# A hybrid HGRN2 / attention / MoE layer: late modulations, the shared expert, the first unit and the order of units

## The chip, the cores and the metric

The kernel runs on one core of one Trainium2 chip. The metric is the device time of one execution in microseconds. Shorter is better.

## The reference

One layer over 256 latent tokens and 256 context tokens of width 1024, all in float32. Only the parts that the change touches matter here:

```python
cond, cond_ctx = silu(c), silu(c_ctx)
mod = cond @ w_ada + b_ada                    # w_ada: 1024 x 6144
sh1, sc1, g1, sh2, sc2, g2 = split(mod, 6)    # 1024 each
h  = modulate(x, sh1, sc1)                    # (LN(x)) * (1 + sc1) + sh1
y  = token_mixer(h, hc, ...)                  # HGRN2 heads, attention heads, merged
x  = layer_norm(alpha * x + g1 * y)
h2 = modulate(x, sh2, sc2)
# 64 experts of width 256, the best 8 per token
routed = sum over experts e: gates[:, e] * (silu(h2 @ Wg[e]) * (h2 @ Wu[e])) @ Wd[e]
shared = (silu(h2 @ w_sh_gate) * (h2 @ w_sh_up)) @ w_sh_down
x  = layer_norm(alpha * x + g2 * (routed + shared))
```

Each expert's weights are 3 MB: gate and up 1 MB each, down 1 MB. The parts of `w_ada` for `g1`, `sh2`, `sc2` and `g2` (4096 columns, 16 MB) are needed late: `g1` after the token mixer, the others from the routing on. They are called the late modulations below.

## The kernel before

**The order on the engines.** TensorE's instructions stand in the order in which the code is written (`manual_schedule`), from the start to the end of the token mixer, and again in the unit loop of the MoE. In the routing between the two, a planner sets TensorE's order, as it does for the other engines everywhere. Weights are loaded by SyncE's queue, in the order of the code; a load waits until its buffer is free.

**The HGRN2 stage** (`Pair`, about 57 to 332 us) works on four pairs of heads. While the scan of one pair runs in small steps (`decays`, `keys`, `states`, `carried`, `squares`, `readout`), the projections of the next pair are fed in between on TensorE (`Feed.pull`). Each projection takes a block of `w_in` of 1024 x 256, which is split into a high part (ScalarE, L335) and a low part (VectorE, L336). Blocks of `w_in` and of the late columns of `w_ada` alternate in the list `todo` and share five buffers of 512 KB (tag `wraw`); a block takes two.

**The late modulations** (`late_sums`, L595) come in 16 chunks of 256 columns, one after each block of a projection. For a chunk ScalarE scales eight pieces of 128 x 256 by `cond` (L601), and GpSimd adds the eight up in three steps (L607 to L609) into `acc`, a tile of 128 x 1024. The sum over the 128 partitions is left to `late_spread` (L611): every four chunks, TensorE multiplies `acc` by ones. For `g1` that is a broadcast to all rows (L617); for the other three it is eight matmuls with one column each (L623), whose stationary operand is a block of `acc` read with a step of eight elements.

In the opening, the early modulations go another way (`ada_parts`, L456): eight narrow matmuls per chunk. Their stationary operand is `cond` of one k, 32 columns wide, and four of them write the four groups of 32 rows of one PSUM bank `pa`, 128 x 256. The sum of the four rows 0, 32, 64 and 96 is the result. The constant `sel2` has a 1 in these rows.

**The routing** (L1141 to L1269) normalizes, transposes and modulates two blocks `t` of 128 tokens, multiplies by the router's weights (L1204), chooses experts on VectorE (`choose`, L1159), ranks the experts by the number of their tokens, and gives each expert a column of its rank. The list `idx` of experts by rank goes to SyncE, which loads weights by it. Four experts (`NSTAT`) stand first whatever their number, so their weights are loaded ahead; they are called static here, the other 60 dynamic.

**The shared expert's gate and up products** (`shared_gu`, L1469) are 16 matmuls for each `t`, two for each of eight k. They are written behind the routing, and the planner may place those of `t` = 0 within it.

**Units.** A unit is up to 128 rows (four tiles of 32) of one or more experts; `_ORDER` (L34) lists the experts of the 29 units. `_program` (L53) writes the steps: `g` gate and up (L1398), `P` places, `t` activation, `G` gather of two units (L1373), `d` down (L1406), `s` and `S` scatter (L1430). The first gather, for unit 0 alone, stands ahead of the shared expert's second half, and unit 0's `g` behind all of the shared expert.

**Slots for weights.** Gate and up weights have six slots in all (`free["g"]`): two for the static ones ahead, two more when the mixer's memory is free, one more when the routing's is, and the shared expert's after its use. An expert holds its slot from its load to the end of the last unit that uses it. `fetch_ahead` (L294) starts the next load in the order of use whenever a slot is given back (`done`, L306).

## Time and profile before

| | |
|---|---|
| Runs of the kernel before | 1134.71, 1138.26, 1138.22 us; median 1138.22 |
| The profiled execution | 1142.01 us, span 1140.1 us |
| Mean granted clock of TensorE | 0.972 |
| Busy share of the span: TensorE, VectorE, ScalarE, GpSimd | 93%, 59%, 40%, 20% |
| HBM read | 293.05 MB, 258 GB/s over the span |

The profiled execution is 3.8 us above the median of the runs, and 1.9 us of its time lie around the span. Busy shares are means over stages with different limits, so they say little by themselves. PE is TensorE, DVE VectorE, ACT ScalarE, POOL GpSimd. A line of the trace gives the kernel's line (L388), the tile written and the tiles read. The text in brackets at the end of a line is the time for which the engine had stood idle before it, and what ended that.

### The profile page before, as it was taken

What the parts mean: (1) busy time and instruction counts of PE and PEld (TensorE: products, weight loads), DVE (VectorE), ACT (ScalarE), POOL (GpSimd) and SP (SyncE); (2) the same over time, 40 slices, a digit from 0 to 9 for tenths busy, and PEclk for the clock granted to TensorE, in tenths of its full rate; (3) what the DMA queues carried; (4) which work ended last, traced back from release to release, by engine and by line L of the source; (5) the groups of instructions that cost most, each with busy time, mean ns of one, the idle gap of its engine ahead of it and who ended that gap; (6) DMA issues with size and microseconds to landing.
All of it is one profiled execution on the core that took longest, in us unless ns stands there. A gap on an engine that the chain in (4) does not pass through costs nothing.

```text
span 1140.1 us, 18936 instructions
## 1 busy us (share of the span) xinstructions
PE 1054.8 (93%) x7232; PEld 735.9 (65%) x7232; DVE 678.0 (59%) x1323; ACT 453.5 (40%) x874; POOL 226.7 (20%) x215
## 2 busy tenths in 40 slices
PE   5998979999899899899998999999998999999994
PEld 3796958879799788788997644444434444454441
DVE  5587695967954786787687333444434344444355
ACT  4584846658543564565533112221112122111120
POOL 1116143342454374460001000000000000000021
PEclk9999989999889999999998899999999899999998
DMA  9944444453576443333695579999999999979991
GB/s 321 295 149 154 143 132 151 126 165 112 183 172 150 114 90 80 89 73 118 232 374 226 222 286 412 399 423 421 425 423 425 422 426 425 423 314 384 426 414 47
DMA packets 115101, 295.36 MB, mean 259 GB/s; under 512 B 7080, under 2 KB 86896, under 8 KB 90432
## 3 DMA queue, kind: packets, MB, share of 16 engines
q1 hardware_dynamic: 113088, 290.46, 67.1%
q0 software_dynamic: 1776, 3.47, 3.3%
q8 instruction: 58, 0.95, 0.3%
q14 instruction: 35, 0.29, 0.1%
q10 hardware_dynamic: 144, 0.20, 0.0%
HBM read 293.05 MB, written 1.05 MB: 258 GB/s over the span
## 4 chain that ended last, share of the span: by engine, by line
PE 48%; DVE 15%; DMA 14%; issue 8%; ACT 6%; POOL 5%; SPq 2%; DVEq 0%; ACTq 0%; POOLq 0%
PE pgu L1398 14%; PE proj L388 10%; PE pdn L1406 6%; DMA gu<-in_w_e_up_dram 5%; PE pxg L1373 4%; DMA gu<-in_w_e_gate_dram 3%; DVE wlo L336 3%; DMA wada<-in_w_ada_dram 3%; DMA G<-in_na_rpb_dram 2%; PE proj L394 2%; PE py L1430 2%; DVE s L728 2%; POOL kl L957 2%; PE pgu L1473 1%; SPq L319 1%
## 5 line engine op out<-in xcount | busy, mean ns | idle before, releaser
L1398 PE MATMUL pgu<-gu,xg 128*32 128x512 f32 (+1 forms) x1456 | 211.7, 601 | 8.8 <-DMA gu<-in_w_e_up_dram 7.3
L336 DVE TENSOR_TENSOR wlo<-wraw,whi 128x1024 fp32r<-128x1024 f32 x102 | 141.8, 1392 | 47.0 <-ACT whi L335 44.9
L1398 PEld LDWEIGHTS pgu<-gu,xg 128*32 128x32 f32 (+1 forms) x1456 | 66.1, 118 | 150.1 <-issue 143.0
L335 ACT CAST whi<-wraw 128x1024 fp32r<-128x1024 f32 x102 | 105.6, 1045 | 47.2 <-PE proj L388 34.5
L1294 DVE SCALAR_TENSOR_TENSOR ac<-ac,gcol,pgu 128x256 f32<-128x256 f32 (+1 forms) x29 | 13.9, 480 | 181.1 <-ACT ac L154 181.1
L1406 PE MATMUL pdn<-dn,at 128*32 128x512 f32 (+3 forms) x740 | 106.0, 589 | 0.0
L388 PE MATMUL proj<-hl,whi 128*128 128x256 f32 (+1 forms) x480 | 103.3, 330 | 0.0
L388 PE MATMUL proj<-hh,whi 128*128 128x256 f32 (+1 forms) x480 | 101.8, 330 | 0.0
L388 PE MATMUL proj<-hh,wlo 128*128 128x256 f32 (+1 forms) x480 | 99.5, 327 | 0.0
L1511 POOL TENSOR_TENSOR end<-cf,mod 128x1024 f32<-128x1024 f32 x1 | 1.9, 1897 | 467.0 <-PE pgu L1398 467.0
L154 ACT ACTIVATE ac<-pgu 128x256 f32<-128x256 f32 (+1 forms) x31 | 11.9, 384 | 203.1 <-PE pgu L1398 203.1
L388 PEld LDWEIGHTS proj<-hh,wlo 128*128 128x128 f32 x480 | 75.8, 193 | 8.8 <-issue 1.4
L388 PEld LDWEIGHTS proj<-hl,whi 128*128 128x128 f32 x480 | 74.3, 193 | 6.6 <-issue 0.7
L388 PEld LDWEIGHTS proj<-hh,whi 128*128 128x128 f32 x480 | 74.1, 191 | 6.9 <-issue 0.5
L1420 ACT CAST rh<-pdn 128x512 fp32r<-128x512 f32 x56 | 32.8, 585 | 101.8 <-PE pdn L1406 94.2
L1421 DVE TENSOR_TENSOR rl<-pdn,rh 128x512 fp32r<-128x512 f32 x56 | 38.6, 691 | 57.6 <-ACT rh L1420 57.5
L1431 DVE TENSOR_TENSOR x<-x,py 128x512 f32<-128x512 f32 x108 | 69.0, 680 | 0.0
L601 ACT ACTIVATE wada<-wada,cond 128x256 f32<-128x256 f32 x128 | 58.5, 500 | 25.1 <-DMA wada<-in_w_ada_dram 25.1
L1406 PEld LDWEIGHTS pdn<-dn,at 128*32 128x32 f32 (+2 forms) x740 | 29.6, 116 | 57.9 <-issue 55.3
L1373 PE MATMUL pxg<-oh,x2h 128*128 128x256 f32 (+1 forms) x240 | 64.1, 302 | 1.4 <-DVE x L1431 1.4
L607 POOL TENSOR_TENSOR wada<-wada 128x1024 f32<-128x1024 f32 x16 | 44.3, 2769 | 97.4 <-ACT wada L601 83.4
L1373 PE MATMUL pxg<-oh,x2l 128*128 128x256 f32 (+1 forms) x240 | 61.3, 289 | 0.0
(389 smaller groups left out, 2030.0 us busy)
## 6 DMA issues: line engine op xcount, KB each, us to landing
gu<-in_w_e_gate_dram SPq DMA_DIRECT2D x64, 1024.0 KB, 15.3
gu<-in_w_e_up_dram SPq DMA_DIRECT2D x64, 1024.0 KB, 17.5
dn<-in_w_e_down_dram SPq DMA_DIRECT2D x61, 1024.0 KB, 17.3
wraw<-in_w_in_dram SPq DMA_DIRECT2D x80, 512.0 KB, 4.6
wada<-in_w_ada_dram SPq DMA_DIRECT2D x48, 512.0 KB, 4.7
wraw<-in_w_branch_a_dram SPq DMA_DIRECT2D x8, 512.0 KB, 3.5
wraw<-in_w_branch_b_dram SPq DMA_DIRECT2D x8, 512.0 KB, 3.8
wraw<-in_w_out_dram SPq DMA_DIRECT2D x8, 512.0 KB, 7.9
```

The costliest lines, as they stand in the source:

```text
L335: nc.scalar.copy(hi, raw)
L336: nc.vector.tensor_sub(lo, raw, hi.bitcast(F32))
L388: nc.tensor.matmul(o, a[:, m * P:(m + 1) * P], b[:, :n], start=first, stop=last)
L394: nc.tensor.matmul(o, b[:, t * P:(t + 1) * P], a, start=first, stop=last)
L601: nc.scalar.activation(w, w, AF.Identity, scale=cond[:, k, 0:1])
L607: nc.gpsimd.tensor_tensor(w0, w0, w1, op=OP.add)
L1373: r = nc.tensor.matmul(pg_, part[:, t, k, :], oh[:, t, :w_], start=(t == 0 and part is x2h), stop=(t == 1 and part is x2l))
L1398: nc.tensor.matmul(o[s:s + w_], xg[:, k, i * P + s:i * P + s + w_], W["g"][j][:, :, k, :], start=(k == 0), stop=(k == KD - 1))
L1406: nc.tensor.matmul(pd[s:s + w_, :ns.stop - ns.start], at[:, jj, s:s + w_], W["d"][j][:, jj, ns], start=(jj == 0), stop=(jj == 1))
L1420: nc.scalar.copy(rh[:used], z)
L1421: last_rl[0] = nc.vector.tensor_sub(rl[:used], z, rh[:used].bitcast(F32)).ins
L1431: nc.vector.tensor_add(to[:, t, ns], to[:, t, ns], py)
```

## The change

The sums of the late modulations go the way of the early ones: eight narrow matmuls into `pa` and one copy by ScalarE per chunk. The three GpSimd additions and the eight ScalarE scalings go. `acc` now has four partial rows instead of 128 partial ones, so the spread uses `quarter`, which is 1 in the rows 0, 32, 64 and 96 and 0 elsewhere, or a column of `sel2`. For the three modulations with one-column matmuls, the copy into `acc` already puts the elements in the order of use, so that the stationary block is contiguous.

```diff
-        w0, w1 = take(None, c)
-        for k in range(KD):
-            w = (w0, w1)[k // 4][:, k % 4, :]
-            nc.scalar.activation(w, w, AF.Identity, scale=cond[:, k, 0:1])
+        pa = ada_parts(take(None, c))
         if c % 4 == 0:
             if c > 8:
                 late_spread()
             sums[1] = pg.tile([P, D], F32, tag="acc", name="acc", bufs=1)
         sums[0] = c
-        nc.gpsimd.tensor_tensor(w0, w0, w1, op=OP.add)
-        nc.gpsimd.tensor_tensor(w0[:, 0:2], w0[:, 0:2], w0[:, 2:4], op=OP.add)
-        nc.gpsimd.tensor_tensor(sums[1][:, c % 4 * 256:(c % 4 + 1) * 256], w0[:, 0], w0[:, 1], op=OP.add)
+        m = c % 4 * 32
+        if c < 12:
+            nc.scalar.copy(sums[1][:, 8 * m:8 * m + 256], pa[:, :256])
+        else:
+            nc.scalar.copy(sums[1].rearrange("p (k m) -> p k m", k=KD)[:, :, m:m + 32],
+                           pa[:, :256].rearrange("p (m k) -> p k m", k=KD))
...
-                nc.tensor.matmul(pr1, ones, acc[:, n * 512:(n + 1) * 512], start=True, stop=True)
+                nc.tensor.matmul(pr1, quarter, acc[:, n * 512:(n + 1) * 512], start=True, stop=True)
...
-                nc.tensor.matmul(pr1[:, k:k + 1], acc.rearrange("p (m k) -> p k m", k=KD)[:, k, :], ones[:, 0:1],
-                                 start=True, stop=True)
+                nc.tensor.matmul(pr1[:, k:k + 1], acc[:, k * P:(k + 1) * P], C("sel2")[:, 0:1], start=True, stop=True)
```

TensorE's written order now runs through the routing too (`order.close()` at its start and the entering behind it are gone). The shared expert's products are written between the routing's own instructions: for `t` = 0 k 0 and 1 behind the first choice, 2 and 3 behind the second block's transposes, 4 to 7 behind the second choice; for `t` = 1 k 0 to 3 in the ranking, and k 4 to 7 behind unit 0's gate and up, which now follows the first gather.

```diff
-    order.close()
     mix.close()
...
+        if t:
+            shared_gu(0, range(2, 4))
         for k in range(KD):
-            on_pe[t] = nc.tensor.matmul(pl[:, t * NE:(t + 1) * NE], h2[k][:, ts], wr[:, k, :], start=(k == 0),
-                                        stop=(k == KD - 1))
+            nc.tensor.matmul(pl[:, t * NE:(t + 1) * NE], h2[k][:, ts], wr[:, k, :], start=(k == 0),
+                             stop=(k == KD - 1))
         choose(t)
+        shared_gu(0, range(4, KD) if t else range(2))
...
+    shared_gu(1, range(1))
     pcn = ps_y()
...
+    shared_gu(1, range(1, 2))
     pix = ps_y()
...
+        if i:
+            shared_gu(1, range(3, 4))
         pj = ps_y() if i else ps_dn()
...
     by_column(0, place, pos)
+    shared_gu(1, range(2, 3))
     by_column(1, gate, gj)
...
-    shared_gu(0, range(3), turned[0].ins)
-    shared_gu(0, range(3, 8), turned[1].ins)
     ohs_ = prepare(0)
-    shared_gu(1, range(8), gather(ohs_))
+    ohg_ = gated(ohs_, 0)
+    gather(ohs_)
+    places(ohg_)
+    outs_ = {0: gate_up(0, ps_dn())}
+    done("g", 0)
+    shared_gu(1, range(4, KD))
     free["g"].append(shs[0])
     fetch_ahead()
-    order.enter_context(tc.manual_schedule(engines={nc.tensor.engine}))
     ats = [act_t(pgs[t], None) for t in range(2)]
-    places(gated(ohs_, 0))
```

The order of the units is new. The static experts 0 to 3 are used in the units 8, 0, 1 and 15 before, and in 10, 3, 0 and 1 after. Expert 4, which has five tiles, is used in the units 21 and 22 before, and in 13 and 20 after. The last unit is the same.

```diff
-_ORDER = [[1, 35], [2, 36], [13, 14], [6, 37], [15, 38, 39], [16, 17], [18, 19], [7, 40], [0, 41], [20, 42, 43], [8, 44], [21, 45, 46], [22, 23], [24, 25], [26, 47, 48], [3, 49], [27, 28], [29, 30], [9, 50], [10, 51], [31, 32], [4], [4, 11], [52, 53, 54, 55], [12, 56], [57, 58, 59, 60], [5], [33, 34], [61, 62, 63]]
+_ORDER = [[2, 35], [3, 36], [13, 37, 38], [1, 39], [6, 40], [14, 15], [16, 41, 42], [17, 18], [19, 43, 44], [20, 21], [0, 45], [22, 46, 47], [23, 24], [4], [25, 26], [7, 48], [27, 28], [29, 30], [31, 32], [33, 34], [4, 8], [9, 49], [10, 50], [51, 52, 53, 54], [11, 55], [56, 57, 58, 59], [5], [12, 60], [61, 62, 63]]
```

## Rows read from the trace of the kernel before

**Rows 1.** Busy time of the engines in the HGRN2 stage and in the units: from:to, length, then the busy us (and instructions) of PE, PEld (weight loads), DVE, ACT and POOL, then the granted clock, the DMA engines' busy share and GB/s.

```profile
56.60:332.00 275.40, 256.45 (x1837) 228.55 (x1836) 215.47 (x341) 183.99 (x389) 105.03 (x76) 0.96 0.47 147
...
656.30:1127.00 470.70, 453.63 (x2997) 204.41 (x2998) 200.61 (x437) 88.22 (x172) 9.10 (x5) 0.99 0.94 391
```

**Rows 2.** Groups of instructions by line, from 56.6 to 332 us: line, engine, operation, tiles, count, then busy us and mean ns of one, then the engine's idle time before them and what ended it.

```profile
L336 DVE TENSOR_TENSOR wlo<-wraw,whi 128x1024 fp32r<-128x1024 f32 x45 | 64.7, 1439 | 16.1 <-ACT whi L335 14.2 <-PE proj L388 1.9
...
L601 ACT ACTIVATE wada<-wada,cond 128x256 f32<-128x256 f32 x128 | 58.5, 500 | 25.1 <-DMA wada<-in_w_ada_dram 25.1
...
L623 PE MATMUL pr<-ones,acc 128*128 128x1 f32 x48 | 11.6, 371 | 0.0
```

**Rows 3.** Waits of TensorE's matmuls from 56 to 332 us: who waited for whom, total us, times, the longest.

```profile
PE psc L749 <- ACT ex L154: 6.6, 3, 4.7
PE pu L775 <- DVE kt L759: 4.6, 3, 2.2
PE pk L745 <- DVE v L691: 3.0, 1, 3.0
```

**Rows 4.** Timeline (start us, length us, what): the split L336 on VectorE once with GpSimd idle, and once beside GpSimd's L607.

```profile
57.69 1.22 DVE L336 TENSOR_TENSOR wlo<-wraw,whi 128x1024 fp32r<-128x1024 f32 x1 [0.17 <-ACT whi L335]
...
109.73 2.38 POOL L607 TENSOR_TENSOR wada<-wada 128x1024 f32<-128x1024 f32 x1 [5.90 <-ACT wada L601]
...
110.62 2.57 DVE L336 TENSOR_TENSOR wlo<-wraw,whi 128x1024 fp32r<-128x1024 f32 x1 [0.62 <-ACT whi L335]
```

**Rows 5.** Busy time of the engines in the four stretches of the HGRN2 stage's time and just behind it in which the granted clock is 0.50 (columns as in rows 1).

```profile
155.47:162.30 6.83, 6.19 (x21) 4.87 (x22) 6.32 (x12) 3.39 (x7) 0.00 (x0) 0.50 1.03 340
216.91:220.32 3.41, 3.41 (x10) 2.62 (x9) 3.41 (x3) 1.03 (x3) 3.16 (x2) 0.50 0.36 119
292.00:298.83 6.83, 4.09 (x24) 4.00 (x25) 6.65 (x14) 4.58 (x9) 0.82 (x2) 0.50 0.56 167
329.55:336.38 6.83, 6.83 (x33) 6.83 (x33) 2.11 (x4) 1.04 (x1) 0.79 (x1) 0.50 0.90 145
```

**Rows 6.** Timeline of TensorE in the opening: two chunks of narrow matmuls (32 instructions) between matmuls of the full width.

```profile
41.97 0.39 PE L539 MATMUL po<-hl,whi 128*128 128x512 f32 x1
42.20 0.40 PE L539 MATMUL po<-hh,wlo 128*128 128x512 f32 x1
42.53 1.93 PE L461 MATMUL pa<-wada,cond 128*32 128x256 f32 x32
44.39 0.51 PE L539 MATMUL proj<-hh,whi 128*128 128x512 f32 x1
```

**Rows 7.** Timeline of TensorE: the spread of one modulation (the stationary blocks have a step), and two matmuls of the MoE with contiguous blocks and what follows them.

```profile
212.75 3.85 PE L623 MATMUL pr<-ones,acc 128*128 128x1 f32 x16
...
777.23 0.38 PE L1357 MATMUL poh<-cf,ohg 128*128 128x128 f32 x2
777.44 0.38 PE L1297 MATMUL pat<-cf,ac 128*128 128x128 f32 x2
```

**Rows 8.** Timeline of TensorE in the routing and up to unit 0: the second block's transposes, the count of tokens per expert (L1222), the first gather, the shared expert's second half, its activation's transposes, unit 0's gate and up.

```profile
617.36 1.04 PE L1194 MATMUL py<-cf,x 128*128 128x128 f32 x8
...
626.08 0.28 PE L1222 MATMUL py<-ones,mask 128*64 128x1 f32 x2 [0.56 <-DVE mask L1180]
...
630.36 0.47 PE L1373 MATMUL pxg<-oh,x2h 128*128 128x128 f32 x1
...
637.25 8.56 PE L1473 MATMUL pgu<-gu,h 128*128 128x256 f32 x32
...
647.29 0.44 PE L1297 MATMUL pat<-cf,ac 128*128 128x128 f32 x2 [1.26 <-DVE ac L1292]
...
656.34 7.18 PE L1398 MATMUL pgu<-gu,xg 128*32 128x512 f32 x64 [1.41 <-issue]
```

**Rows 9.** Timeline of VectorE and ScalarE in the routing: the second block's normalization, its router scores' sigmoid, and the list of experts.

```profile
614.16 1.23 DVE L1188 TENSOR_SCALAR x<-x,mv,rs 128x1024 f32<-128x1024 f32 x1 [0.66 <-POOL rs L189]
...
622.75 0.22 ACT L154 ACTIVATE sco<-pdn 128x64 f32<-128x64 f32 x1 [2.14 <-PE pdn L1204]
...
628.22 0.21 DVE L1244 CAST idx<-py 1x64 int32<-1x64 f32 x1
```

**Rows 10.** The issue of the first dynamic expert's up weights in the timeline of SyncE's queue; then DMA issues (what, queue, count, KB each, median us from issue to landing): that one's (629 to 632.9 us), and those of the late columns of `w_ada` (79 to 130 us).

```profile
630.32 0.34 SPq L241 DMA_DIRECT2D gu<-in_w_e_up_dram  x1
...
gu<-in_w_e_up_dram SPq DMA_DIRECT2D x1, 1024.0 KB, 7.9
...
wada<-in_w_ada_dram SPq DMA_DIRECT2D x7, 512.0 KB, 3.7
```

**Rows 11.** Timeline of TensorE: gate and up of unit 4, of unit 11 (its start), of unit 12 and of unit 14 (in two pieces each).

```profile
720.54 4.93 PE L1398 MATMUL pgu<-gu,xg 128*32 128x512 f32 x44 [1.37 <-DMA gu<-in_w_e_up_dram]
...
831.14 1.04 PE L1398 MATMUL pgu<-gu,xg 128*32 128x512 f32 x8
...
844.69 1.07 PE L1398 MATMUL pgu<-gu,xg 128*64 128x512 f32 x2
847.23 7.08 PE L1398 MATMUL pgu<-gu,xg 128*64 128x512 f32 x30 [1.46 <-DMA gu<-in_w_e_up_dram]
...
878.31 2.14 PE L1398 MATMUL pgu<-gu,xg 128*32 128x512 f32 x6
884.29 9.53 PE L1398 MATMUL pgu<-gu,xg 128*32 128x512 f32 x58 [3.85 <-DMA gu<-in_w_e_up_dram]
```

More of the change, by code (lines that the diff above doesn't have):

```diff
@@ L634, in build @@
     pg2 = gl.enter_context(tc.tile_pool(name="pg2", bufs=2, reuse_waits="tile"))
+    quarter = pg.tile([P, P], F32, name="quarter")
+    nc.vector.tensor_copy(quarter, C("sel2")[:, 0:1].to_broadcast([P, P]))
     zm = pg.tile([P, 768], F32, name="zm")
@@ L1148, in build, with shared_gu @@
     pl = ps_dn()
-    on_pe, turned = [None, None], [None, None]
+    pgs = [ps_gu(), ps_gu()]
+    gu, dn = shw
+    def shared_gu(t, ks):
+        for k in ks:
+            for q in range(2):
+                nc.tensor.matmul(pgs[t][:, q * FE:(q + 1) * FE], h2[k][:, t * P:(t + 1) * P], gu[:, q, k, :],
+                                 start=(k == 0 and q == 0), stop=(k == KD - 1 and q == 1), skip_group_check=True)
     rt = {n: pb_.tile([P, 2] + d, F32, name=n) for n, d in (
@@ L1193, in build @@
             for i in range(4):
-                turned[t] = nc.tensor.transpose(pt[:, i * P:(i + 1) * P], x2[:, t, kk + i, :], ident)
+                nc.tensor.transpose(pt[:, i * P:(i + 1) * P], x2[:, t, kk + i, :], ident)
             for i in range(4):
@@ L1372, in gather @@
                 for part in (x2h, x2l):
-                    r = nc.tensor.matmul(pg_, part[:, t, k, :], oh[:, t, :w_],
-                                         start=(t == 0 and part is x2h), stop=(t == 1 and part is x2l))
+                    nc.tensor.matmul(pg_, part[:, t, k, :], oh[:, t, :w_],
+                                     start=(t == 0 and part is x2h), stop=(t == 1 and part is x2l))
             if k % 2 == 0:
@@ L1382, in gather @@
             xgs[u] = xg
-        return r.ins
     def pieces(u):
@@ L1390, in pieces, with gate_up @@
                 yield j, s, w_
-    def gate_up(u):
+    def gate_up(u, o=None):
         i = prep[u][0]
         xg = xgs.pop(u)
-        o = ps_gu()
+        o = ps_gu() if o is None else o
         for k in range(KD):
@@ L1462, in build @@
     fetch_ahead()
-    gu, dn = shw
-    pgs = [ps_gu(), ps_gu()]
-    def shared_gu(t, ks, after):
-        with tc.issue_after(after):
-            for k in ks:
-                for q in range(2):
-                    r = nc.tensor.matmul(pgs[t][:, q * FE:(q + 1) * FE], h2[k][:, t * P:(t + 1) * P], gu[:, q, k, :],
-                                         start=(k == 0 and q == 0), stop=(k == KD - 1 and q == 1),
-                                         skip_group_check=True)
-        return r.ins
-    shared_gu(0, range(3), turned[0].ins)
-    shared_gu(0, range(3, 8), turned[1].ins)
-    ohs_ = prepare(0)
-    shared_gu(1, range(8), gather(ohs_))
+    ohs_ = prepare(0)
+    ohg_ = gated(ohs_, 0)
[4 more added lines that the diff above has]
+    shared_gu(1, range(4, KD))
     free["g"].append(shs[0])
     fetch_ahead()
-    order.enter_context(tc.manual_schedule(engines={nc.tensor.engine}))
     ats = [act_t(pgs[t], None) for t in range(2)]
-    places(gated(ohs_, 0))
     for t in range(2):
@@ L1500, in build @@
     ohg_ = gated(ohs_, 0)
-    outs_, ats_, downs, pys, last_rl = {}, {}, {}, {}, [None]
+    ats_, downs, pys, last_rl = {}, {}, {}, [None]
     bc2 = xf = None
@@ L1543, in build @@
     end = None
-    for op, i in steps:
+    assert steps[0] == ("g", 0)
+    for op, i in steps[1:]:
         if op == "G":
```

## The prediction

> **What bounds the kernel now.** I read the busy time by stage first, then in each stage what TensorE waits for, and last the timelines around the edits. TensorE is the engine that is nearly always busy [rows 1]: 256.5 of 275.4 us in the HGRN2 stage, 453.6 of 470.7 in the units. So a microsecond counts if it is TensorE's own work on the written order, TensorE's idle time, or a stretch at the lower clock. In the units the DMA engines are as full (0.94) [rows 1]: there TensorE and the stream of weights bound together, and an earlier start pays only if the stream moves too.
>
> In the HGRN2 stage TensorE idles for 275.4 - 256.5 = 18.9 us. The three largest waits are for VectorE, and for a ScalarE exponential that itself follows VectorE; they make 14.2 us [rows 3]. VectorE is late where GpSimd adds: the split that takes 1.22 us alone takes 2.57 us beside L607, and its mean over 45 is 1.44 [rows 2, 4]. GpSimd is busy for 105 us of this stage [rows 1], most of it with the sums that the change removes.
>
> **The change part by part: the late modulations.**
>
> Removed: the 16 x 3 additions on GpSimd, and 58.5 us of ScalarE [rows 2]. 16 copies of 128 x 256 come instead; at no more than the 0.50 us of a scaling of the same size [rows 2] they are 8 us at most. Neither engine is the bound here, so this is worth only what TensorE's idle time shrinks by.
>
> Added to TensorE: 16 chunks of narrow matmuls. Two such chunks stand between full-width matmuls in the opening [rows 6]. These follow each other every 0.23 us (41.97 to 42.20), so without the chunks the next would have begun at 42.43; it began at 44.39, and the 0.11 us that it lasts longer than its neighbours (0.51 against 0.40) is the way back to full width. That is 2.07 us for two chunks, of which 2 x 0.93 = 1.86 are the 32 instructions and the rest the edges. A chunk alone has both edges: 0.93 + 0.21 = 1.14, which I round to 1.2 us. 16 x 1.2 = **+19.2 us**, all in TensorE's written order (from 14.9 without edges up to 22).
>
> The spreads: 16 one-column matmuls with stepped stationary blocks take 3.85 us, 0.24 each; two with contiguous blocks occupy 777.23 to 777.44, 0.105 each [rows 7]. All three spreads last 11.6 us [rows 2]; at 0.11 they take 48 x 0.11 = 5.3: **-6.3 us** (0 to -6.5).
> Here the Trainium skill speaks against the change: "TensorE: Matmul & The Clock Gate", section "LDWEIGHTS (loading the stationary operand)", prices a weight load by its number of columns alone, so a contiguous block would load no faster than a stepped one. By that the saving is 0 and the sum 6.3 us higher. The 0.24 against 0.105 us above differ although both have 128 columns, so I go by the rows.
>
> Given back: the idle time. All three waits of [rows 3] hang on VectorE's queue, and without the additions it no longer stretches. I take 14 of the 18.9 us back; the least is 0 (TensorE may find the next link of the same chain late), the most 18.9. **-14 us.**
>
> The clock falls to 0.50 in four stretches [rows 5]. Two (155, 292 us) come right behind or inside the long idle times, and cost half of their busy time: (6.19 + 4.09) / 2 = 5.1. Two (217, 330) begin as the 3.85 us of one-column matmuls end, and cost (3.41 + 6.83) / 2 = 5.1. I take 4 of the first pair (its stalls go) and 2.5 of the second (the spreads halve, but stay): **-6.5 us** (0 to -10.2).
>
> Sum of this stage: 19.2 - 6.3 - 14 - 6.5 = **-7.6 us**. Its ends: nothing given back and no faster spread +22, everything -16.
>
> Two new waits I cost at nothing. TensorE now waits in line for a chunk of `w_ada`, and behind it stand the projection and the scan's steps, for which VectorE and ScalarE wait. The cover: such a load lands 3.7 us after its issue [rows 10], and its buffer is free when the chunk before is consumed, one chunk in 275.4 / 16 = 17 us earlier on average [rows 1]. And `pa` takes a turn in the three PSUM buffers of the scan; the projection's matmuls behind it cover its copy.
>
> **Routing and unit 0.** The second block is normalized at 614.16 + 1.23 = 615.4 [rows 9], but its transposes begin at 617.36 [rows 8], since TensorE was in the shared expert's products. In the new order only two k of these stand ahead of them, so I let the router's result come 2 us earlier (bounds 0 and 3): the sigmoid at 620.8 instead of 622.75 [rows 9], the choice as long behind it as now (626.08 - 622.75 = 3.3) at 624.1. Written ahead of the count are five k (4 to 7, and one of the second half). Half of the shared expert, 8 k, took 8.4 us up to 645.65, partly at the lower clock; I take 0.85 us a k, 4.3 us, so the count begins at 620.8 + 4.3 = 625.1, 1 us earlier than now. From there the list of experts takes 2.35 us (626.08 to 628.43) and is there at 627.5 [rows 8, 9]. The three k written in the rest of the ranking are 2.6 us, of which 1.3 fall into TensorE's waits: the gather still begins near 630.5.
>
> Unit 0 can begin when the first dynamic expert's weights land. That is 630.32 + 7.9 = 638.2 now [rows 10]; with the list 0.9 us earlier, 637.3. The gather ends by then, so the transfer decides. Unit 0: 637.3 + 7.2 = 644.5. The shared expert's other four k: 3.4. The stretch from its end to unit 0 (645.65 to 656.34, 10.7 us with the 1.26 and 1.41 us of idle [rows 8]) stays: 644.5 + 3.4 + 10.7 = 658.6. Now unit 0 ends at 656.34 + 7.18 = 663.5: 4.9 us later. Unit 0's activation is then long done, which takes away the 1.7 us that TensorE waits for it behind unit 0. **-6.6 us**; at least -3 (choice not earlier, lower clock up to unit 0), at most -9.5.
>
> **The order of units.** TensorE waits for weights in unit 4 for 1.4 us; unit 12 runs from 844.69 to 854.3, 2.4 us longer than unit 0's 7.2; unit 14 from 878.31 to 893.8, 8.3 us longer, the lower clock behind its wait included [rows 8, 11]. Together 12.1 us. The stream's pace between the last two: unit 12 needs the 26th dynamic expert, which let it go on at 847.23, unit 14 the 31st, 884.29: 7.41 us each. The new list needs the 24th in unit 11, the 26th in unit 12, the 29th in 14 and the 31st only in 15. Unit 11 began at 831.14 and would at about 831.1 - 6.6 - 1.4 = 823.1; the 24th expert is there at 847.2 - 2 x 7.41 - 6.6 = 825.8, if the stream moves with unit 0's slots: 2.7 us of wait. Unit 12, some 13.5 us later, begins at 839.3 and has its 26th at 840.6: 1.3 more. Units 14 and 15 have theirs in time. Unit 2 now needs three dynamic experts, and the third one's slot comes free only with unit 1's end: about 1.5 us. With edges 6 us remain of 12: **-6 us** (-10 to +8: expert 4 holds one of six slots from unit 13 to 20, and each unit with three or four new experts asks for 22 or 30 us of stream).
>
> **Sum.** -7.6 - 6.6 - 6 = -20.2 us. The profiled execution, 1142.0, would become 1121.8; it lies 3.8 above the median of the runs, 1138.2, so I say **1118**.
>
> **The rivals.**
> - *The scan's stage gives everything back* (-16 instead of -7.6): 1138.2 - 28.6 = 1110, and 1103 with the routing and the order at their good ends (-9.5 and -10). For it: all large waits sit beside GpSimd's additions. Against: chains of short instructions keep some waits whatever the load. 0.14.
> - *TensorE's new work eats the stage.* 19.2 us are certain, the idle time returned is not. If 10 of the 29 us of idle time and low clock come back, the stage is 19.2 - 6.3 - 10 = +3, the total -9.7: 1128; if none, 1138. 0.17.
> - *The new order starves.* With 10 us more of waits than I count: 1128 to 1135. For it: DMA share 0.94 [rows 1]. Against: three of four static experts leave their slots by unit 3. 0.06.
> - *Slower: TensorE stands in line for `w_ada`.* ScalarE waited 25.1 us in total for these loads [rows 2]. Then the wait cost little; now it would stop TensorE. Price per chunk up to 3.7 us [rows 10], 16 chunks up to 59 us: 1177 at the worst, 1148 with half. It decides from 20.2 / 16 = 1.26 us per chunk. Against: the buffer is free a chunk ahead. 0.08.
>
> **How the numbers follow.** The forecast (1108 to 1127) has 0.55. The range 1104 to 1134 leaves out the slower rival, the tail of the second and the best of the first, together under 0.2. About 0.3%, 3.4 us, is what a measurement here can tell from no change. Faster (under 1134.8): the forecast, the first rival, and most of the second and third, 0.87; within it 0.05; slower 0.08.
>
> **What would show it.** Right: in the HGRN2 stage narrow matmuls of about 19 us on TensorE, idle time near 5 instead of 19 us, splits at 1.22 us, and spreads of about 1.8 us; unit 0 ends 5 us nearer to the first transposes; waits for weights in the units near 6 us. Wrong: waits of `pa` for `w_ada`, an idle time over 10 us in the stage, spreads still at 0.24 us a matmul, or a wait over 4 us in any unit.

## The result, and the profile after

The changed kernel takes 1111.7 us (median of four runs, 1108.6 to 1112.55); the kernel before took 1138.24 beside it. The ratio is 0.9753, with an interval of 0.9726 to 0.978: 26.5 us less, where 20.2 were forecast (1118 us). The profiled execution took 1111.24 us, its span is 1109.3 us, and the mean granted clock rose from 0.972 to 0.989.

From the page of the kernel after: busy time by engine, and TensorE's busy share and clock in 40 slices.

```profile
PE 1049.4 (95%) x7488; PEld 726.1 (65%) x7488; DVE 637.4 (57%) x1320; ACT 414.5 (37%) x766; POOL 139.5 (13%) x167
...
PE   4999999999999889899998999999999999999994
...
PEclk9999999999999999999998999999999999999998
```

The table of stretches says where the 30.8 us between the two spans went. The stretches are cut at the same instructions in both kernels: the first projection of the HGRN2 stage (L388 in both), the first matmul behind that stage, the routing's first transposes, the start of unit 1's gate and up, and the end. Columns are those of [rows 1]. First the kernel before:

```profile
56.63:330.18 273.55, 254.60 (x1829) 226.73 (x1828) 213.83 (x338) 183.96 (x389) 105.03 (x76) 0.97 0.47 147
330.18:608.27 278.09, 260.84 (x1922) 239.72 (x1922) 200.38 (x371) 140.46 (x243) 98.28 (x104) 0.98 0.53 145
608.27:673.40 65.13, 58.78 (x328) 43.63 (x332) 30.68 (x111) 15.86 (x34) 1.56 (x2) 0.87 0.65 256
673.40:1140.10 466.70, 438.86 (x2870) 195.31 (x2862) 203.15 (x437) 85.34 (x166) 12.90 (x8) 0.98 0.93 387
```

And the kernel after:

```profile
56.52:316.96 260.44, 259.48 (x2085) 222.83 (x2084) 173.02 (x334) 144.58 (x281) 17.92 (x28) 1.00 0.50 155
316.96:592.54 275.58, 258.16 (x1922) 237.06 (x1922) 200.29 (x371) 140.82 (x244) 98.10 (x104) 0.99 0.54 146
592.54:651.00 58.46, 54.34 (x328) 37.53 (x332) 31.01 (x115) 15.87 (x34) 1.57 (x2) 0.94 0.72 296
651.00:1109.30 458.30, 435.25 (x2870) 197.84 (x2862) 202.92 (x433) 85.37 (x166) 12.93 (x8) 0.99 0.95 392
```

The four differences are -13.1, -2.5, -6.7 and -8.4 us. In the first stretch TensorE does 256 instructions more and is busy 4.9 us longer, and yet the stretch is shorter, because its idle time (length less busy) falls from 18.95 to 0.96 us. VectorE's column is the other thing to see: with practically the same number of instructions (338 and 334) it is busy 40.8 us less, though the change removes no work of that size from VectorE. In the second and third stretch TensorE runs the same number of instructions in less busy time: there it is the clock.

The groups of the HGRN2 stage that answer to [rows 2], from 56 to 317 us:

```profile
L336 DVE TENSOR_TENSOR wlo<-wraw,whi 128x1024 fp32r<-128x1024 f32 x45 | 55.1, 1224 | 20.6 <-ACT whi L335 18.7 <-PE proj L388 1.9
L461 PE MATMUL pa<-wada,cond 128*32 128x256 f32 x256 | 17.1, 385 | 0.0
...
L623 PE MATMUL pr<-cm,acc 128*128 128x1 f32 x48 | 5.7, 249 | 0.0
L623 PEld LDWEIGHTS pr<-cm,acc 128*128 128x128 f32 x48 | 5.6, 192 | 0.8 <-ACT whi L335 0.8
L608 ACT COPY acc<-pa 128x256 f32<-128x256 f32 x12 | 4.4, 367 | 10.2 <-PE pr L623 4.6 <-PE pr L617 3.6 <-PE pa L461 2.0
```

The split's mean fell from 1439 to 1224 ns, which is the 1.22 us that it takes with GpSimd idle [rows 4]. The narrow matmuls wait for nothing ("0.0" behind the bar): TensorE never stands in line for `w_ada`. The one wait of TensorE that the list of waits for the same stretch still has, where [rows 3] had 14.2 us:

```profile
PE pr L617 <- DVE v L693: 1.0, 1, 1.0
```

The timeline of TensorE in the routing, which answers to [rows 8] (L1204 is the second block's transposes, L1236 the count, L1391 the gather, L1415 unit 0's gate and up, L1157 the shared expert's last four k; L1375 is the places, of unit 0 at 619.95, and at 642.47 as the first instruction of the unit loop):

```profile
600.80 1.04 PE L1204 MATMUL py<-cf,x 128*128 128x128 f32 x8
...
609.60 0.39 PE L1236 MATMUL py<-ones,mask 128*64 128x1 f32 x4
...
616.32 0.33 PE L1391 MATMUL pxg<-oh,x2h 128*128 128x128 f32 x1
...
619.95 0.41 PE L1375 MATMUL poh<-cf,ohg 128*128 128x128 f32 x2
620.28 8.22 PE L1415 MATMUL pdn<-gu,xg 128*32 128x512 f32 x64
628.43 3.72 PE L1157 MATMUL pgu<-gu,h 128*128 128x256 f32 x16
...
642.47 0.41 PE L1375 MATMUL poh<-cf,ohg 128*128 128x128 f32 x2 [1.41 <-issue]
```

And the units that still wait for weights, from the same timeline, answering to [rows 11] (units 2, 12 and 26):

```profile
665.66 7.03 PE L1415 MATMUL pgu<-gu,xg 128*32 128x512 f32 x58 [0.17 <-DMA gu<-in_w_e_up_dram]
...
823.94 7.05 PE L1415 MATMUL pgu<-gu,xg 128*64 128x512 f32 x30 [1.29 <-DMA gu<-in_w_e_up_dram]
...
1043.10 5.42 PE L1415 MATMUL pgu<-gu,xg 128*128 128x512 f32 x12 [1.15 <-DMA gu<-in_w_e_up_dram]
```

They make 2.6 us of idle time. The longest wait of before, 3.85 us in unit 14 with the lower clock behind it, is gone.

### The profile page after: what moved, and what is told of

Its sections match the earlier page's. It is cut to its first block, busy times and chain, and to the rows that moved or that the text cites. A ratio compares the mean times of both kernels' runs of the same rounds, so it can differ in the third digit from the quotient of the medians.

```text
span 1109.3 us, 19272 instructions
## 1 busy us (share of the span) xinstructions
PE 1049.4 (95%) x7488; PEld 726.1 (65%) x7488; DVE 637.4 (57%) x1320; ACT 414.5 (37%) x766; POOL 139.5 (13%) x167
## 4 chain that ended last, share of the span: by engine, by line
PE 39%; DMA 12%; issue 7%; DVE 6%; POOL 4%; ACT 3%; SPq 0%; DVEq 0%; ACTq 0%; POOLq 0%
PE pgu L1415 13%; PE pdn L1423 6%; PE proj L388 5%; DMA dn<-in_w_e_down_dram 5%; PE pxg L1391 4%; DMA gu<-in_w_e_up_dram 3%; DMA G<-in_na_rpb_dram 2%; PE proj L394 2%; PE py L1447 2%; DMA gu<-in_w_e_gate_dram 2%; POOL kl L959 1%; PE pgu L1157 1%; PE o L394 1%; PE po L1019 1%; POOL G L941 1%
## 5 line engine op out<-in xcount | busy, mean ns | idle before, releaser
L1415 PE MATMUL pgu<-gu,xg 128*32 128x512 f32 (+2 forms) x1392 | 200.8, 593 | 2.6 <-DMA gu<-in_w_e_up_dram 2.6
L336 DVE TENSOR_TENSOR wlo<-wraw,whi 128x1024 fp32r<-128x1024 f32 x102 | 132.8, 1303 | 49.3 <-ACT whi L335 47.3
L1415 PEld LDWEIGHTS pgu<-gu,xg 128*32 128x32 f32 (+2 forms) x1392 | 64.7, 117 | 135.3 <-issue 128.2
L1423 PE MATMUL pdn<-dn,at 128*32 128x512 f32 (+2 forms) x740 | 106.0, 589 | 0.0
L388 PE MATMUL proj<-hh,whi 128*128 128x256 f32 (+1 forms) x480 | 101.6, 329 | 0.0
L388 PE MATMUL proj<-hl,whi 128*128 128x256 f32 (+1 forms) x480 | 101.0, 324 | 0.0
L388 PE MATMUL proj<-hh,wlo 128*128 128x256 f32 (+1 forms) x480 | 98.1, 323 | 0.0
L388 PEld LDWEIGHTS proj<-hh,wlo 128*128 128x128 f32 x480 | 74.5, 190 | 8.5 <-issue 1.4
L388 PEld LDWEIGHTS proj<-hh,whi 128*128 128x128 f32 x480 | 72.5, 189 | 11.4 <-issue 4.2
L388 PEld LDWEIGHTS proj<-hl,whi 128*128 128x128 f32 x480 | 72.8, 189 | 6.2 <-issue 0.7
L1423 PEld LDWEIGHTS pdn<-dn,at 128*32 128x32 f32 (+1 forms) x740 | 29.6, 116 | 57.8 <-issue 55.3
L1391 PE MATMUL pxg<-oh,x2h 128*128 128x256 f32 (+1 forms) x240 | 60.9, 292 | 2.0 <-DVE x L1448 1.5
L1391 PE MATMUL pxg<-oh,x2l 128*128 128x256 f32 (+1 forms) x240 | 58.2, 280 | 0.0
L1447 PE MATMUL py<-rh,ohs 128*128 128x512 f32 x108 | 50.0, 463 | 4.5 <-DVE x L1448 3.3
L1394 ACT ACTIVATE xg<-pxg,mod 128x256 f32<-128x256 f32 (+1 forms) x60 | 33.4, 557 | 43.9 <-PE pxg L1391 43.8
```

The lines of the kernel that those rows point to most:

```text
L336: nc.vector.tensor_sub(lo, raw, hi.bitcast(F32))
L388: nc.tensor.matmul(o, a[:, m * P:(m + 1) * P], b[:, :n], start=first, stop=last)
L1391: nc.tensor.matmul(pg_, part[:, t, k, :], oh[:, t, :w_], start=(t == 0 and part is x2h), stop=(t == 1 and part is x2l))
L1394: nc.scalar.activation(xg[:, k, :w_], pg_, AF.Identity, bias=mod2[:, 0, k:k + 1], scale=mod2[:, 1, k:k + 1])
L1415: nc.tensor.matmul(o[s:s + w_], xg[:, k, i * P + s:i * P + s + w_], W["g"][j][:, :, k, :], start=(k == 0), stop=(k == KD - 1))
L1423: nc.tensor.matmul(pd[s:s + w_, :ns.stop - ns.start], at[:, jj, s:s + w_], W["d"][j][:, jj, ns], start=(jj == 0), stop=(jj == 1))
```

## Experiments

All are the changed kernel with one part different. "The stage" is the HGRN2 stage as cut above: 273.6 us before, 260.4 after.

### One part undone at a time

**The late sums as before.**

```diff
-        pa = ada_parts(take(None, c))
+        w0, w1 = take(None, c)
+        for k in range(KD):
+            w = (w0, w1)[k // 4][:, k % 4, :]
+            nc.scalar.activation(w, w, AF.Identity, scale=cond[:, k, 0:1])
...
+        nc.gpsimd.tensor_tensor(w0, w0, w1, op=OP.add)
+        nc.gpsimd.tensor_tensor(w0[:, 0:2], w0[:, 0:2], w0[:, 2:4], op=OP.add)
+        nc.gpsimd.tensor_tensor(sums[1][:, c % 4 * 256:(c % 4 + 1) * 256], w0[:, 0], w0[:, 1], op=OP.add)
```

> The changed kernel with the late modulations summed as before (scalings on ScalarE, additions on GpSimd), all else changed. If the gains of the parts add up, the 15.7 us by which the routing begins earlier are lost and nothing else is: 1126 to 1129 us, TensorE idle for 17 us or more between 56 and 332 us, and the units as fast as in the changed kernel. If the parts overlap (the stream of weights gives the later stage its own bound), 1112 to 1120 us.

Measured: 1125.84 us, ratio 0.9882 (0.9852 to 0.9912), 14.1 above the changed kernel. The stage's row:

```profile
56.50:331.00 274.50, 258.76 (x1830) 230.92 (x1830) 213.77 (x338) 184.00 (x389) 105.42 (x76) 0.96 0.47 147
```

Idle time (15.7 us, where 17 or more were expected), the half clock (five stretches in the stage) and VectorE's 213.8 busy us are all back. The stage is 14.1 us longer, as much as the medians differ, so the parts add up. But this run undoes two things at once: the additions are back on GpSimd, and the spreads' blocks have their step of eight elements again. What the step alone costs, the stepped blocks below show: 9.5 of the 14.1 us. The additions on GpSimd in place of the narrow matmuls make the other 1125.84 - 1121.2 = 4.6 us.

**The order of units as before.**

```diff
-_ORDER = [[2, 35], [3, 36], [13, 37, 38], [1, 39], ...
+_ORDER = [[1, 35], [2, 36], [13, 14], [6, 37], ...
```

> The changed kernel with the order of units of before. If the order itself takes the waits for weights away, they come back in units 4, 12 and 14, 8 us or more in all, and the time is 1119 to 1123 us. If the earlier start and the earlier slots of unit 0 were enough, waits stay under 4 us and the time is 1111 to 1115 us.

Measured: 1118.66 us, ratio 0.9824 (0.9793 to 0.9856): the order is worth 7 us. Unit 1 to the end takes 464.1 instead of 458.2 us, and the waits for weights, in the list of TensorE's waits from 600 us on, are 6.0 us instead of 2.6 (8 or more were expected), the longest again in unit 14:

```profile
PE pgu L1415 <- DMA gu<-in_w_e_up_dram: 6.0, 3, 4.0
```

**Stepped stationary blocks in the spreads.**

```diff
-        if c < 12:
+        if True:
...
-                nc.tensor.matmul(pr1[:, k:k + 1], acc[:, k * P:(k + 1) * P], C("sel2")[:, 0:1], start=True, stop=True)
+                nc.tensor.matmul(pr1[:, k:k + 1], acc.rearrange("p (m k) -> p k m", k=KD)[:, k, :], C("sel2")[:, 0:1],
+                                 start=True, stop=True)
```

> The changed kernel with the spreads' stationary blocks stepped again, same matmuls otherwise. By the rows (0.24 against 0.11 us a matmul) the three spreads take 6 us more; if the lower clock behind them comes from these stretches, it is back behind the first and the last spread and costs up to 5 us more: 1118 to 1123 us. If a load costs by its number of columns alone, the time stays at 1110 to 1113 us. If the steps cost but the clock stays, 1117 to 1119 us.

Measured: 1121.2 us, ratio 0.9845 (0.9816 to 0.9873), 9.5 above the changed kernel. The stage, the three stretches in it and just behind it with the granted clock at 0.50, and then the two lines of the spreads:

```profile
56.50:326.00 269.50, 268.54 (x2086) 231.50 (x2084) 173.22 (x334) 144.90 (x281) 17.93 (x28) 0.99 0.49 150
214.56:217.97 3.41, 3.41 (x9) 2.63 (x9) 0.00 (x0) 0.00 (x0) 0.00 (x0) 0.50 1.03 347
282.83:286.24 3.41, 3.41 (x19) 3.41 (x18) 0.00 (x0) 0.37 (x1) 0.00 (x0) 0.50 1.00 338
327.20:330.61 3.41, 3.41 (x18) 3.41 (x18) 0.61 (x2) 0.91 (x1) 2.93 (x4) 0.50 0.92 256
```

```profile
L623 PE MATMUL pr<-cm,acc 128*128 128x1 f32 x48 | 11.8, 376 | 0.0
L623 PEld LDWEIGHTS pr<-cm,acc 128*128 128x128 f32 x48 | 11.6, 334 | 0.8 <-ACT whi L335 0.8
```

The step costs 11.8 - 5.7 = 6.1 us in the spreads themselves, and about 5.1 us (half of three stretches of 3.41) behind them: each of the three runs of one-column matmuls (they end at 213.26, 281.59 and 326.14 us) is followed by the half clock within 1.3 us, with no idle time of TensorE between. That makes 11.2 us in the profiled execution, which was itself 2.6 us above the median of its runs; the medians differ by 9.5. In the kernel before, two of the three runs were followed so [rows 5], and the middle one, at 279.85 us, was not. The weight load takes 334 ns with a step and 192 without, with 128 columns in both.

**Unit 0's gate and up behind all of the shared expert, as before.**

```diff
     gather(ohs_)
-    places(ohg_)
-    outs_ = {0: gate_up(0, ps_dn())}
-    done("g", 0)
     shared_gu(1, range(4, KD))
```

> The changed kernel with unit 0's gate and up back behind all of the shared expert. TensorE's own work is the same, and the wait for the first dynamic expert is then covered by the shared expert. If unit 0's early slots feed the stream, its two slots open some 15 us later, waits for weights come back in the first units, and the time is 1115 to 1119 us. If the stream had enough slots anyway, 1110 to 1113 us.

Measured: 1111.52 us, ratio 0.976 (0.9731 to 0.979): no difference. From the routing's first transposes to unit 1 it takes 60.3 instead of 58.5 us, and the 1.7 us for which TensorE waits behind unit 0 for its activation are back. But the rest takes 457.3 instead of 458.2 us: there TensorE waits 2.1 instead of 2.6 us for weights, which came meanwhile, so half of the gain is given back.

**None of the shared expert inside the ranking.** All of its second half stands behind unit 0.

```diff
-    shared_gu(1, range(1))
     pcn = ps_y()
...
-    shared_gu(1, range(4, KD))
+    shared_gu(1, range(KD))
```

> The changed kernel with no shared products inside the ranking: all eight k of the second half behind unit 0. If the written pieces fill waits of TensorE in the ranking, it idles there again for 1 us or more, 1.5 to 3 us more work stand behind unit 0, and the time is 1113 to 1115 us. If they delay the list of experts and so the stream, the list is 1.5 us or more earlier and the time is 1108 to 1111 us.

Measured: 1116.24 us, ratio 0.9792 (0.9761 to 0.9824), 4.5 slower and over the 1113 to 1115 us that had been expected. TensorE idles in three short gaps in the ranking (0.63, 0.46 and 0.46 us), and then the granted clock is 0.50, over the gather and the start of unit 0 and once more at unit 1's gather:

```profile
612.98:623.22 10.24, 10.24 (x53) 7.28 (x55) 5.29 (x20) 2.35 (x6) 0.00 (x0) 0.50 0.97 402
647.12:650.53 3.41, 3.41 (x16) 3.41 (x17) 0.95 (x4) 1.06 (x2) 0.00 (x0) 0.50 0.43 180
```

Half of both is 6.8 us; from the first transposes to unit 1 it takes 65.0 instead of 58.5 us. So the pieces of the shared expert in the ranking are worth their place for the clock, and not for the list of experts, which comes 1.0 us earlier without them.

### What in the old sums held TensorE up

**ScalarE's scalings alone**, on a tile that nobody reads:

```diff
+        for k in range(KD):
+            s_ = scr[:, k % 4 * 256:(k % 4 + 1) * 256]
+            nc.scalar.activation(s_, s_, AF.Identity, scale=cond[:, k, 0:1])
```

> The changed kernel with eight scalings of 128 x 256 on ScalarE per chunk, on a scratch tile that nobody reads: ScalarE's 58 us are back, GpSimd's are not. If GpSimd's additions were the cause, TensorE stays idle for under 4 us between 56 and 332 us and the time is 1110 to 1115 us. If ScalarE's load was, VectorE waits longer for high parts and exponentials, TensorE idles for 8 us or more, and the time is 1119 us or more.

Measured: 1109.77 us, ratio 0.9731 (0.9702 to 0.976). ScalarE is as busy as before the change, and the stage doesn't notice:

```profile
56.50:317.00 260.50, 259.29 (x2084) 222.64 (x2083) 175.13 (x340) 187.51 (x399) 19.34 (x28) 1.00 0.50 155
```

**GpSimd's additions alone**, on a tile that nobody reads, with nothing that they wait for:

```diff
+        nc.gpsimd.tensor_tensor(scr, scr, scr, op=OP.add)
+        nc.gpsimd.tensor_tensor(scr[:, :512], scr[:, :512], scr[:, 512:], op=OP.add)
+        nc.gpsimd.tensor_tensor(scr[:, :256], scr[:, :256], scr[:, 256:512], op=OP.add)
```

> The changed kernel with three additions of the old sizes on GpSimd per chunk, on a scratch tile of zeros that nobody reads: GpSimd's load is back, ScalarE's is not, and no buffer waits for it. If GpSimd's additions were what held VectorE up and through it TensorE, splits of 2 us and more are back, TensorE idles for 8 us or more between 56 and 332 us, and the time is 1119 to 1130 us. If ScalarE's load or the held buffers were the cause, the time is 1110 to 1115 us.

Measured: 1146.0 us, ratio 1.0063 (1.0043 to 1.0083), slower than any expectation. The planner put all the additions in one row, from 48 to 131 us, in front of GpSimd's own small steps of the scan. TensorE idles for 29 us in the stage. From the list of its waits there:

```profile
PE psc L757 <- DVE v L699: 14.6, 1, 14.6
PE po L791 <- POOL kb L774: 6.9, 1, 6.9
PE pk L753 <- DVE ex L742: 4.1, 1, 4.1
```

The second is a wait for GpSimd's queue, not for a slow instruction. The other two, 18.7 us, are waits for VectorE, which is busy for 53.2 of the 56 us from 74 to 130, beside 53.5 us of GpSimd, and a split in it takes 2.57 us instead of 1.22:

```profile
74.00:130.00 56.00, 29.34 (x185) 23.00 (x184) 53.20 (x48) 15.83 (x29) 53.46 (x33) 0.79 0.30 94
```

```profile
105.54 2.57 DVE L336 TENSOR_TENSOR wlo<-wraw,whi 128x1024 fp32r<-128x1024 f32 x1
```

No buffer of `w_ada` is held here, and ScalarE has no scalings. So additions that run beside VectorE's instructions are enough by themselves to make VectorE late and TensorE wait. What they cost at the moments of the old sums, this run does not show.

**The same additions, each chunk's held back** until the chunk's copy into `acc` is there, by a small instruction that reads it:

```diff
+        at_ = 8 * m if c < 12 else m
+        nc.gpsimd.tensor_tensor(scr[:, :32], sums[1][:, at_:at_ + 32], sums[1][:, at_:at_ + 32], op=OP.mult)
+        nc.gpsimd.tensor_tensor(scr, scr, scr, op=OP.add)
...
```

> As the kernel with three additions per chunk on GpSimd, but each chunk's begin with a small one that reads the chunk's copy in acc, so that they come when the chunk does and not all in one row early. If the additions hold VectorE up by running beside it, its splits are stretched again (mean over 1.35 us against 1.22), TensorE idles for 8 us or more in the HGRN2 stage and the time is 1118 to 1128 us. If only the row of early additions did it, by standing ahead of the scan's own instructions on GpSimd, 1110 to 1115 us.

Measured: 1113.39 us, ratio 0.9768 (0.9735 to 0.9801). The stage takes 262.7 us, with 2.3 us of idle time:

```profile
56.50:319.20 262.70, 260.44 (x2085) 222.95 (x2084) 180.97 (x333) 143.22 (x278) 93.61 (x91) 1.00 0.49 153
```

GpSimd is nearly as busy as in the old sums, but VectorE is only 8 us longer busy than without the additions, not 41, and its splits take 1225 ns: at these moments, behind a chunk's matmuls, the additions seldom meet VectorE's long instructions. The two traces show it: with the old sums back, splits and additions run side by side for 26.7 us (15 splits with an addition beside them for over three tenths of their time, 1.96 us on the mean, against 1.23 for the rest), here for 4.3 us (five such splits, 1.22 us). At these moments GpSimd's load costs TensorE 1.3 us of idle time.

**GpSimd busy without reading**: five memsets for each chunk in place of the additions.

```diff
+        for _ in range(5):
+            nc.gpsimd.memset(scr, 0.0)
```

> As the paced additions, with five memsets of 128 x 1024 per chunk in their place: GpSimd is occupied for about as long (some 5 us per chunk), but reads nothing. If it is what GpSimd reads that holds VectorE up, the splits stay at 1.22 to 1.28 us and the time is 1110 to 1115 us. If GpSimd's queue being busy is enough, the time is that of the paced additions.

Measured: 1112.6 us, ratio 0.9762 (0.973 to 0.9794), no difference. Since the paced additions cost next to nothing either, the time can't tell the two expectations apart; VectorE's column can, 174.9 us here and 181.0 there:

```profile
56.50:317.00 260.50, 259.54 (x2086) 222.88 (x2085) 174.89 (x334) 143.93 (x280) 98.28 (x122) 1.00 0.49 154
```

**The old sums with the buffers of `w_ada` given back early.** ScalarE writes six of the eight scaled pieces into a tile of their own; GpSimd adds as many columns as before, in four instructions.

```diff
-            nc.scalar.activation(w, w, AF.Identity, scale=cond[:, k, 0:1])
+            nc.scalar.activation(scr[:, k, :] if k < 6 else w, w, AF.Identity, scale=cond[:, k, 0:1])
...
-        nc.gpsimd.tensor_tensor(w0, w0, w1, op=OP.add)
+        nc.gpsimd.tensor_tensor(scr[:, 4:6], scr[:, 4:6], w1[:, 2:4], op=OP.add)
+        nc.gpsimd.tensor_tensor(scr[:, 0:2], scr[:, 0:2], scr[:, 2:4], op=OP.add)
```

> e1_sums_back once more (late sums as before the change, the rest changed), but ScalarE writes six of the eight scaled pieces into a tile of their own, and GpSimd adds from there: a column of GpSimd's work as before (1792 columns a chunk, now in four instructions), at the same moments, but one of the two buffers of w_ada is given back as soon as ScalarE has read it, and the other after the first addition of 512 columns. Theory A (GpSimd's additions stretch VectorE's instructions at the moments when VectorE is late): nothing changes: the HGRN2 stage stays at 271 to 277 us with 12 to 17 us of idle TensorE and stretches at the lower clock, total 1122 to 1129. Theory B (the held buffers make the next blocks of w_in land late, and so VectorE's split): idle under 5 us and the half clock behind the stalls gone, stage 255 to 262, total 1106 to 1114. The split's mean stays above 1400 ns by A, and by B says nothing.

Measured: 1119.58 us, ratio 0.9836 (0.9806 to 0.9866), between the two theories: 6.3 below the old sums and 7.9 above the changed kernel. The spreads' blocks have their step here too, so the run to hold beside it is the one with stepped blocks: the additions on GpSimd, with the buffers given back early, took no longer than the narrow matmuls (1119.58 against 1121.2 us).

```profile
56.50:323.00 266.50, 255.60 (x1829) 228.60 (x1827) 202.38 (x339) 184.03 (x388) 108.39 (x92) 0.96 0.49 152
```

Of the old sums' 15.7 us of idle time 10.9 stay. So buffers given back early help, but do not remove the stalls; VectorE is still 29 us busier than in the changed kernel. The other form of the additions also moved their moments: splits and additions run side by side for 18.6 us instead of 26.7. So the 4.8 us between can't be given to the buffers alone.

### Two attempts at more

**The count of overflowing units ahead of unit 0.**

```diff
     places(ohg_)
+    nov = overflow()
     outs_ = {0: gate_up(0, ps_dn())}
```

> The changed kernel with the count of overflowing tokens, and the 1.41 us in which TensorE reads it into a register, ahead of unit 0's gate and up, where TensorE waits some 1.2 us for the first dynamic expert's weights. If the read is hidden there, 1 us less: 1110 to 1111 us, and no idle 1.41 us behind the shared expert. If the wait for the weights only follows it, no change: 1111 to 1113 us.

Measured: 1114.34 us, ratio 0.9764 (0.974 to 0.9789). It brought no gain: TensorE now waits ahead of unit 0 for VectorE (1.5 us), the granted clock is 0.50 from 621.27 to 628.10, in unit 0, and unit 2 waits 2.9 us for weights instead of 0.17.

**Work for TensorE ahead of the routing's first transposes**, where it idles for 2.5 us: three matmuls that nobody reads.

```diff
             pt = ps_y() if t else ps_mm("pt")
+            for _ in range(0 if t or kk else 3):
+                nc.tensor.matmul(pt, ident, wr.rearrange("p k e -> p (k e)"), start=True, stop=True)
```

> The changed kernel with three idle-filling matmuls of 128 x 512 (their result is overwritten) ahead of the routing's first transposes, where TensorE stands idle for 2.5 us and the clock falls behind it. If the idle time is what lets the clock fall, it stays at 1.00 there, the routing is 1 to 3 us shorter and the time is 1108.5 to 1111 us. If the matmuls come late or the clock falls anyway, 1111 to 1114 us.

Measured: 1112.34 us, ratio 0.9751 (0.9725 to 0.9777), no gain. The half clock at 593.80 is gone, and from the first transposes to the unit loop it takes 48.6 instead of 49.9 us. But the fillers run over the moment at which the transposes could start, 594.15 us, when ScalarE's normalization of their input ends. TensorE's timeline:

```profile
592.23 2.84 PE L1204 MATMUL pt<-wr,cf 128*128 128x512 f32 x6 [0.52 <-DVE yg L1098]
594.91 1.04 PE L1206 MATMUL pt<-cf,x 128*128 128x128 f32 x8
```

That costs 0.7 us. The rest of the gain goes to another stretch at half clock, from 644.75 to 648.16 in unit 1's gather, which the changed kernel doesn't have. The transposes begin 2.2 us later in their stretch (277.8 against 275.6 us), but most of that is not the fillers: a third stretch, long before them, costs 1.7 us, and the run with the old order of units, whose code is the same up to the routing, has it as well (from 504.90 us).

```profile
504.80:508.22 3.42, 3.42 (x17) 2.57 (x13) 0.85 (x2) 0.40 (x1) 0.00 (x0) 0.50 0.00 0
644.75:648.16 3.41, 3.41 (x16) 3.41 (x17) 0.94 (x3) 1.11 (x2) 0.00 (x0) 0.50 0.86 360
```

## Why the prediction was right, and where its terms were off

**The HGRN2 stage** was forecast at -7.6 us and gave -13.1, or -15.6 with the stretch behind it, into which most of the fourth half-clock stretch of [rows 5] falls.
- *Narrow matmuls, +19.2*: 17.1 us busy for 256. The sum of the stage closes with 18: -18.0 (idle) - 7.1 (clock, the part inside the stage) - 5.9 (spreads) + x = -13.1. The term was 1 us too large.
- *Spreads, -6.3*: 11.6 to 5.7 us, -5.9. Here the Trainium skill ("TensorE: Matmul & The Clock Gate", section "LDWEIGHTS (loading the stationary operand)"), which prices a load by its columns alone, is contradicted: 334 against 192 ns for 128 columns, and 0.25 against 0.12 us a matmul. The measurement decides.
- *Idle time, -14*: 18.0 of 18.95 came back. *Clock, -6.5*: all four stretches of [rows 5] went, 10.2. These are the mis-sized terms, 4.0 and 3.7 us of the 8 that the stage gave beyond the forecast. The prediction kept 2.6 us of the half clock behind the spreads because they "halve, but stay". The stepped blocks showed that this was the point: none of the three spreads of 1.84 to 1.95 us was followed by the half clock, and all three of 3.86 to 3.97 were.

The reason given for the idle time, that VectorE is late where GpSimd adds, stands on the rows of VectorE: 213.8 us busy with the old sums, 202.4 with the buffers freed, 181.0 with paced additions, 174.9 with memsets and 173.0 after, and the idle time of TensorE goes the same way: 15.7, 10.9, 2.3, 1.0 and 1.0. It is not GpSimd's busy time, which is 105, 108, 94, 98 and 18 us, nor ScalarE's. What counts is whether GpSimd's additions run beside VectorE's long instructions: the row of additions that held no buffer made VectorE late and TensorE wait, and the paced ones, which seldom met the splits, didn't. So this way is shown. That the held buffers have a part as well is likely from the run that gave them back early, but how much of the idle time is theirs stays open: no run had the old moments with the buffers entirely free.

The terms can also be put together by the two parts of the change. Moving the sums costs TensorE 17.9 us and gives back 18.0 of idle time and the 5.1 of clock beside it [rows 5]; the contiguous blocks give 5.9 us and the other 5.1 of clock, and cost TensorE nothing. The runs say the same: 4.6 us for the one, 9.5 for the other. So most of what this stage gave is the blocks', not the moving. Whether the old sums with contiguous blocks, and with their buffers given back early, would be as fast as the changed kernel, no run shows.

The Trainium skill ("SBUF — State Buffer", section "Who interferes with whom") says that VectorE and GpSimd share one pair of ports as an exclusive lock. The trace agrees where it could be tried: the split beside L607 [rows 4] began at 110.62, and L607 ended at 109.73 + 2.38 = 112.11; 1.22 us later is 113.33, and the split ended at 113.19, as if it had stood still until L607 was done.

**Rival "the stage gives everything back"** is therefore what happened there (-15.6 against its -16), and the measured 1111.7 us lies nearer to its 1110 than to the 1118 that was said. The rivals that saw the stage eaten up or the wait for `w_ada` fell: the idle time came back, and no narrow matmul waited for a load.

**Routing and unit 0** were forecast at -6.6 and gave -6.7, but by other steps: that the numbers agree is luck.
- The count comes 609.60 - 592.54 = 17.1 us behind the first transposes, against 626.08 - 608.27 = 17.8 [rows 8]: 0.75 earlier, where 1 was forecast.
- The gather begins 23.8 us behind them, against 22.1; it was to begin at the same time. The pieces of the shared expert in front of it cost more than the gaps they fill.
- Unit 0 ends 36.0 us behind them, forecast 644.5 - 608.3 = 36.2. The loop begins at 49.9, against 656.34 + 7.18 - 608.27 = 55.25 before, where unit 0 was the last thing ahead of it: 5.3 earlier, forecast 4.9.
- The step that is wrong is the cause. Of the 6.7 us, 4.4 are busy time, with 328 instructions in both (58.78 and 54.34): the half clock over the first gather is gone, which [rows 8] didn't name. With a bare ranking it came back at once, and 6.5 of the 6.7 us with it. The place of unit 0 was worth nothing to the total.

The half clock over the first gather, in the kernel before:

```profile
629.92:640.16 10.24, 10.24 (x42) 9.58 (x42) 3.81 (x13) 3.14 (x6) 0.00 (x0) 0.50 0.93 362
```

**The order of units** was forecast at -6 and is worth 5.9 us in its stretch and 7 in the medians. Of the three waits forecast, 1.5 in unit 2, 2.7 in unit 11 and 1.3 in unit 12, the trace has 0.17, none and 1.29 us of idle time; one of 1.15 in unit 26 was not forecast. By the length from first to last matmul, in which the prediction counted, units 2, 11 and 12 took 8.23, 7.24 and 9.41 us, against 7.05 to 7.09 without a wait: 1.2, 0.2 and 2.3 us. So the sum was near, and its places were not. The wait of 3.85 us and the lower clock behind it went as forecast.

**The sum** in the profiled executions is -30.8 us in the spans, and in the medians -26.5: the profiled execution of before lay 3.8 us above its median, as the prediction had counted, and that of after 0.5 below.

## What to carry to other kernels

Work on an engine that is far from full can still set the pace, through another engine: look at whether the same instructions of a third engine (here VectorE's splits, 1224 against 1439 ns) get longer beside it, and move the work to where, or when, it doesn't meet them. Moving it to the fullest engine can pay, but price it by itself: here 17 us of narrow matmuls on TensorE bought back 18 us of its idle time and 5 of its clock, while reading the stationary blocks without a step was worth 9.5 us. Idle gaps and slow runs of one-column matmuls can cost twice, once themselves and once in the lower clock behind them, and pieces of independent work placed into the gaps of a chain can then be worth more than the gap (in the ranking 6.5 us, for two gaps of 1.1 us together). When an experiment gives an engine's load back, look at when the load runs: the same additions cost 34 us in one early row and 1.7 us behind each chunk's copy.

## What had not been expected

- A stationary block with a step of eight elements loads in 334 ns, a contiguous one in 192, and 16 one-column matmuls of the one kind (3.86 to 3.97 us) were followed by 3.41 us at half clock all three times, although TensorE never stood still; 16 of the other (1.84 to 1.95 us) were not.
- 76 us of memsets on GpSimd left VectorE nearly where it was (174.9 against 173.0 us busy), and additions at the same moments added 8 us, while the 87 us of additions of the old sums, at theirs, added 41.
- Three filler matmuls removed a stretch at half clock of 6.83 us and gained nothing: they were 0.7 us in the way themselves, and another stretch at half clock came up behind the routing.
